# A hybrid encoder trunk: the input projection moved ahead and done in Strassen blocks

## Chip, cores and metric

The kernel runs on one core of a Trainium2 chip. The metric is device time in microseconds, as the median of three runs.

## What is computed

Two layers over 1024 tokens of 1024 features, float32. In each layer `h = RMSNorm(x)`, and one matrix product `proj = h @ w_in` (1024 x 6912) gives ten parts:

```
qA 512, kA 128, vA 128, zA 512, uB 512, vB 512, zB 512, qM 512, zM 512, gate logits 3 x 1024
yA = attention(rope(norm(qA)), rope(norm(kA)), vA) * silu(zA)      8 query heads of 64, 2 key heads, all 1024 keys
yB = uB * (W_s LayerNorm(vB) + b) * silu(zB)                       mixing within chunks of 128 tokens, 4 groups
yM = attention(qM, 256 memory keys and values) * silu(zM)          4 heads of 128
x  = x + (sum over n of sigmoid(gate_n) * (y_n @ w_br[n])) @ w_out  y_n 512 wide, w_br[n] 512 x 1024
```

After the last layer comes one more RMSNorm. The memory's keys and values are `RMSNorm(mem) @ w_mem_kv` in each layer.

## The kernel before

Every float32 operand is split into a high part (rounded to float32r) and a low part (the rest), and each product is three passes on TensorE, high x high, high x low, low x high (`mm3`, L107 to L110). The split takes a ScalarE copy and a VectorE subtraction (`split`, L112); for weights a ScalarE copy and, as a rule, GpSimd subtractions (`split_w`, L129). All DMAs go out on SyncE's queue.

The normed tokens stand transposed in SBUF as `hT`, 1024 features by 1024 tokens, high and low, in two token halves. A feature block of 128 columns is 8 K tiles x 3 passes of 512 tokens per half (`feat`, `feat_steps`); Q, K and V are made with rows as tokens and 256 weight columns moving (`token_proj`, `query`).

A layer runs in this order:

1. Branch A (`gqa`, L375): keys and values for the eight token tiles, then a loop over 32 units (key head, query tile, head pair) of four chunks each. A chunk `G` weighs values (`weigh`), turns the probabilities of chunk G+2 (`turn`), and in its second half computes scores and softmax of the unit after next (`scores`: product, maximum on VectorE, exponent on ScalarE, reciprocal on VectorE, scaling on GpSimd). Between them `fill` runs products that wait for nothing of the attention: the gate paths of branches A and B, kept in DRAM (`fillers`, L229). `owed` sets how many: 1.5 per chunk. The queries of the next tile are made in the same loop.
2. `merge` (L289): for each of 8 feature blocks the branch's output times `w_br`, into a two-bank tile `up = psS()`, of which there are two, and with it the tanh of the gate logits of a later block (`logits`, L275).
3. Branch M (`cross`, L622): memory keys and values, queries in the single bank `psM`, eight units of scores, turning, values; then its merge.
4. Branch B (`spatial`, L761), then its merge.
5. `out_proj` (L851), which for layer 0 also norms and turns the next layer's tokens.

The order on TensorE within an attention is that of the program (`in_order`); elsewhere a planner sets it by priorities. PSUM has two two-bank tiles `psS`, two banks `psT` for transposes, and one bank each `psM` and `psA`.

## Time and profile before

| What | Value |
|---|---|
| three runs, median (lowest to highest) | 2226.77 us (2225.23 to 2227.15) |
| profiled execution: span from first to last instruction | 2222.3 us (the page gives no other time for it) |
| TensorE busy | 2160.5 us, 97%, 11528 products |
| VectorE, ScalarE, GpSimd busy | 993.9, 865.3, 792.9 us |
| mean granted clock of TensorE | 0.998 |
| DMA | 133.61 MB, mean 60 GB/s |

A busy time is the union of an engine's instructions. TensorE's are pipelined: one lasts longer than the step to the next, so a busy TensorE isn't one at its peak, and the step has to be read from the starts. "Idle before" is the time that an engine stood still just before a group, with what ended it.

### The profile page before, as it was taken

To read this page: it belongs to the slowest core of one execution; us is meant where nothing else is said; L and a number is where in the kernel's file an instruction comes from. 1 tells how busy PE (TensorE), PEld (TensorE's weight loads), DVE (VectorE), ACT (ScalarE), POOL (GpSimd) and SP (SyncE) were. 2 spreads that over 40 slices of the span, in tenths; PEclk is the share of its full clock that TensorE was granted. 3 is DMA by queue.
4 is the path that set the end of the run, shared out by engine and by line. 5 is a ranking of instruction groups with operands and counts; after the bars stand their busy time and mean duration, and the time that the engine had idled before them with its cause. 6 is when DMAs were issued, how large, how long until landed. Compare 5 with 4: busy or idle time off the path is not lost.

```text
span 2222.3 us, 29304 instructions
## 1 busy us (share of the span) xinstructions
PE 2160.5 (97%) x11528; PEld 1844.7 (83%) x11528; DVE 993.9 (45%) x1670; ACT 865.3 (39%) x1679; POOL 792.9 (36%) x876
## 2 busy tenths in 40 slices
PE   8999999999999999999999999999999999999998
PEld 7889888788888888788788888888888888887887
DVE  6566676501334126414345676764013332264232
ACT  5566666511334111212245666664123341112132
POOL 6445454422133222422254454453221332223133
PEclk9999999999999999999999999999999999999999
DMA  4101010211211111312221110112123111212122
GB/s 167 53 29 40 28 39 20 95 48 57 77 47 58 48 54 34 122 47 97 94 87 39 38 39 25 39 34 77 47 66 90 31 55 46 58 67 95 41 100 78
DMA packets 111929, 133.61 MB, mean 60 GB/s; under 512 B 5168, under 2 KB 90160, under 8 KB 111792
## 3 DMA queue, kind: packets, MB, share of 16 engines
q1 hardware_dynamic: 111792, 131.75, 18.8%
q8 instruction: 90, 1.47, 0.3%
q14 instruction: 47, 0.39, 0.1%
HBM read 114.95 MB, written 16.78 MB: 59 GB/s over the span
## 4 chain that ended last, share of the span: by engine, by line
PE 84%; DVE 6%; ACT 4%; DMA 2%; POOL 2%; issue 2%; SPq 0%; POOLq 0%; ACTq 0%; DVEq 0%
PE psS L108 18%; PE psS L109 18%; PE psS L110 17%; PE psM L108 5%; PE psA L512 4%; PE psM L110 4%; PE psM L109 4%; PE psT L498 4%; PE psS L478 2%; PE psS L479 2%; DMA raw<-in_w_in_dram 1%; POOL wt L135 1%; ACT b L484 1%; DVE pT L115 1%; PE psA L108 1%
## 5 line engine op out<-in xcount | busy, mean ns | idle before, releaser
L135 POOL TENSOR_TENSOR wt<-raw,wt 128x512 fp32r<-128x512 f32 x286 | 385.0, 1370 | 704.8 <-ACT wt L132 703.1
L108 PE MATMUL psS<-hh,wt 128*128 128x512 f32 x896 | 354.4, 395 | 3.9 <-ACT th L286 3.9
L110 PE MATMUL psS<-hh,wt 128*128 128x512 f32 x896 | 350.3, 391 | 0.0
L109 PE MATMUL psS<-hl,wt 128*128 128x512 f32 x896 | 349.4, 390 | 0.0
L132 ACT CAST wt<-raw 128x1024 fp32r<-128x1024 f32 x164 | 172.3, 1053 | 323.2 <-PE psS L109 276.2
L108 PE MATMUL psS<-wt,hh 128*128 128x256 f32 (+1 forms) x736 | 253.7, 345 | 0.9 <-DVE th L318 0.6
L109 PE MATMUL psS<-wt,hh 128*128 128x256 f32 (+1 forms) x736 | 247.5, 336 | 0.5 <-POOL wt L135 0.5
L115 DVE TENSOR_TENSOR pT<-psT,pT 128x512 fp32r<-128x512 f32 x288 | 197.1, 687 | 112.1 <-ACT pT L114 111.2
L110 PE MATMUL psS<-wt,hl 128*128 128x256 f32 (+1 forms) x736 | 246.7, 335 | 0.0
L114 ACT CAST pT<-psT 128x512 fp32r<-128x512 f32 x288 | 167.9, 588 | 134.8 <-PE psT L498 96.3
L108 PEld LDWEIGHTS psS<-hh,wt 128*128 128x128 f32 x896 | 168.6, 188 | 44.9 <-ACT th L286 12.4
L286 ACT ACTIVATE th<-psS 128x512 f32<-128x512 f32 x96 | 57.2, 596 | 379.7 <-PE psS L110 379.7
L108 PE MATMUL psM<-hh,wt 128*128 128x512 f32 x480 | 195.8, 408 | 8.1 <-ACT th L263 6.7
L110 PEld LDWEIGHTS psS<-hh,wt 128*128 128x128 f32 x896 | 168.5, 188 | 36.2
L109 PEld LDWEIGHTS psS<-hl,wt 128*128 128x128 f32 x896 | 168.9, 188 | 33.1
L110 PE MATMUL psM<-hh,wt 128*128 128x512 f32 x480 | 188.2, 392 | 0.4 <-POOL wt L135 0.4
L109 PE MATMUL psM<-hl,wt 128*128 128x512 f32 x480 | 188.4, 392 | 0.0
L318 DVE SCALAR_TENSOR_TENSOR th<-th,psS 128x512 f32<-128x512 f32 x64 | 41.1, 684 | 312.7 <-PE psS L110 312.7
L486 POOL TENSOR_SCALAR b<-b,sums 128x1024 f32<-128x1024 f32 x128 | 144.3, 1128 | 98.8 <-DVE sums L485 83.8
L512 PEld LDWEIGHTS psA<-pT,b 128*128 128x128 f32 x1024 | 155.1, 190 | 26.1 <-DVE pT L115 4.4
L481 DVE TENSOR_REDUCE nm<-psS 128x1 f32<-128x1024 f32 x128 | 155.5, 1218 | 35.1 <-PE psS L479 34.9
L512 PE MATMUL psA<-pT,b 128*128 128x256 f32 x1024 | 165.7, 283 | 5.7 <-DVE pT L115 3.1
(191 smaller groups left out, 4009.2 us busy)
## 6 DMA issues: line engine op xcount, KB each, us to landing
raw<-in_w_in_dram SPq DMA_DIRECT2D x108, 512.0 KB, 3.8
raw<-in_w_br_dram SPq DMA_DIRECT2D x24, 512.0 KB, 3.4
raw<-in_w_mem_kv_dram SPq DMA_DIRECT2D x16, 512.0 KB, 3.5
raw<-in_w_out_dram SPq DMA_DIRECT2D x16, 512.0 KB, 3.7
b<-in_x_dram SPq DMA_DIRECT2D x12, 512.0 KB, 6.6
sz_a<-th SPq DMA_DIRECT2D x16, 256.0 KB, 2.7
uz_b<-th SPq DMA_DIRECT2D x16, 256.0 KB, 2.2
b<-sz_a SPq DMA_DIRECT2D x16, 256.0 KB, 3.7
```

Source lines behind the costliest of these rows:

```text
L108: in_order(nc.tensor.matmul(ps, sh, mh, start=start, stop=False))
L109: in_order(nc.tensor.matmul(ps, sh, ml, start=False, stop=False))
L110: in_order(nc.tensor.matmul(ps, sl, mh, start=False, stop=stop))
L114: nc.scalar.copy(h, src)
L115: nc.vector.tensor_tensor(out=l, in0=src, in1=f32(h), op=ALU.subtract)
L132: nc.scalar.copy(h, raw)
L135: op = lo_eng[0].tensor_tensor(out=l[:, k], in0=raw[:, k], in1=f32(h[:, k]), op=ALU.subtract)
L286: nc.scalar.activation(ts[th], gp[:, s], AF.Tanh, scale=0.5)
L481: nc.vector.tensor_reduce(out=nm, in_=S, axis=AX.X, op=ALU.max, negate=True)
L486: nc.gpsimd.tensor_scalar(out=p, in0=p, scalar1=sums, scalar2=1.0, op0=ALU.mult, op1=ALU.mult)
L498: in_order(nc.tensor.transpose(pt[:, (2 * j + h) * P:(2 * j + h + 1) * P], pp[k, h][:, kt * P:(kt + 1) * P], ident))
L512: in_order(nc.tensor.matmul(acc[:, :256], V[g][:, 2 * c + j], pv[:, j * 256:(j + 1) * 256], start=c + i + j == 0, stop=c == 3 and i + j == 2))
```

## The change

The whole input projection of a layer comes first. It takes two feature blocks (256 columns), both halves of K (b11, b21 hold the first token half, b12 and b22 the second) and both token halves as a 2 x 2 block matrix and makes seven products in place of eight. Differences of the tokens (t1 to t4) are made and split once per layer in `Tokens.put`, sums of weight quarters per pair in `combos`. A pair uses banks X, Y (one `psS`) and Z (`psM` or `psA`); two results are summed within a bank, others by VectorE from PSUM. The results go to DRAM. While the products run, `qkv` reads Q, K and V back for each token tile, turns, norms, rotates and stores them, and `spatial` does branch B; each `yield n` waits n products. Memory keys and values of both layers are made at the start. Then come the cross attention with branch B's projection as filler, the attention with branch M's, branch A's projection by itself, and the output projection. TensorE keeps the order of the program throughout (`pe`).

```diff
-FINISH = {70: (0, 0), 74: (1, 0), 78: (0, 1), 82: (1, 1), 116: (2, 0), 120: (3, 0)}
+FINISH = {110: (0, 0), 112: (1, 0), 115: (0, 1), 118: (1, 1), 121: (2, 0), 124: (3, 0)}
+ORDER = (1, 6, 2, 7, 5, 4, 3)
+EARLY = (1, 2, 6, 7, 5, 4, 3)
+MOVING = {1: "b11", 2: "b21", 3: "b22", 4: "t4", 5: "t1", 6: "t2", 7: "t3"}
+AHEAD = 7
+    slp = ctx.enter_context(tc.tile_pool(name="slp", bufs=16))
     wp = ctx.enter_context(tc.tile_pool(name="wp", bufs=8))
     rawp = ctx.enter_context(tc.tile_pool(name="rawp", bufs=2))
+    b2p = ctx.enter_context(tc.tile_pool(name="b2p", bufs=14))
+    def split_w(raw, lo=None):
+        w = wt([P, 2] + [int(n) for n in raw.shape[1:]])
+        tc.stamp_issue_order_token(nc.scalar.copy(w[:, 0], raw).ins, "cast")
+        (lo or nc.gpsimd).tensor_tensor(out=w[:, 1], in0=raw, in1=f32(w[:, 0]), op=ALU.subtract)
+        return w[:, 0], w[:, 1]
...
+    class Tokens:
...
+        def put(self, y, tt):
...
+            tensor(out=t3, in0=pts[1], in1=b12, op=ALU.subtract)
+            tensor(out=t1, in0=b12, in1=b11[0], op=ALU.subtract)
+            tensor(out=t1, in0=t1, in1=b11[1], op=ALU.subtract)
+            tensor(out=t2, in0=pts[1], in1=t1, op=ALU.subtract)
+            tensor(out=t4, in0=b21[0], in1=t2, op=ALU.subtract)
+            tensor(out=t4, in0=t4, in1=b21[1], op=ALU.add)
+            for name, t in (("t2", t2), ("t3", t3), ("t1", t1), ("t4", t4)):
+                h, l = self.get(name)
+                split(h[:, :, c], l[:, :, c], t, lo=nc.gpsimd)
+    def combos(raw, order):
...
+        a11, a12, a21, a22 = quad(0, 0), quad(0, 1), quad(1, 0), quad(1, 1)
...
+            elif p == 6:
+                s = slab((P, 4, 4, P), F32)
+                tensor(out=s[:, 0], in0=a21, in1=a22, op=ALU.add)
+                tensor(out=s[:, 1], in0=s[:, 0], in1=a11, op=ALU.subtract)
+                yield op(s[:, 1])
+            elif p == 7:
+                tensor(out=s[:, 2], in0=a11, in1=a21, op=ALU.subtract)
+                yield op(s[:, 2])
+            elif p == 5:
+                yield op(s[:, 0])
+            else:
+                tensor(out=s[:, 3], in0=a12, in1=s[:, 1], op=ALU.subtract)
+                yield op(s[:, 3])
+    class Block:
...
+        def product(self, p, w, h):
+            def mm(ps, start):
+                for k in range(4):
+                    mm3(ps, w[0][:, k], w[1][:, k], h[0][:, k], h[1][:, k], start and k == 0, k == 3, skip=True)
+            def add(ps, t, o):
+                with tc.high_priority(offset=400):
+                    nc.vector.tensor_tensor(out=o, in0=ps, in1=t, op=ALU.add)
+            if p == 1:
+                t = psS()
+                self.X, self.Y = t[:, :512], t[:, 512:]
+                mm(self.X, True)
+                self.c1 = b2()
+                with tc.high_priority(offset=400):
+                    nc.scalar.copy(self.c1, self.X)
+            elif p == 6:
+                mm(self.Y, True)
+                self.u2 = b2()
+                add(self.Y, self.c1, self.u2)
+            elif p == 2:
+                mm(self.X, False)
+                self.use(0, 0, self.X, True)
+            elif p == 7:
+                mm(self.Y, False)
+                self.u3 = b2()
+                add(self.Y, self.c1, self.u3)
+            elif p == 5:
+                zbank[0] = 1 - zbank[0]
+                self.Z = psM() if zbank[0] else psA()
+                mm(self.Z, True)
+                add(self.Z, self.u3, self.u3)
+                self.use(1, 1, self.u3, False)
+            elif p == 4:
+                mm(self.Y, False)
+                add(self.Y, self.c1, self.c1)
+                self.use(1, 0, self.c1, False)
+            else:
+                mm(self.Z, False)
+                add(self.Z, self.u2, self.u2)
+                self.use(0, 1, self.u2, False)
+    def in_proj(L, H, between, side):
+        seq = [(0, 1), (1, 1), (0, 2), (1, 2)]
+        seq += [(b, p) for b in (0, 1) for p in EARLY[2:]]
+        seq += [(b, p) for b in range(2, len(todo)) for p in ORDER]
...
+        for i, (b, p) in enumerate(seq):
+            prepare(i + 1 + AHEAD)
+            state[b].product(p, ops.pop((b, p)), H.get(MOVING[p]))
...
+    def branch(L, n, y, merged, first):
+        raws = [fetch(w_br[L.l, n], 0, 512, 4)]
+        for d0 in range(0, KT, 2):
+            W = [split_w(raws[-1][:, :, j * P:(j + 1) * P]) for j in (d0 % 4, d0 % 4 + 1)]
...
+            for th in range(2):
+                for j in range(2):
...
+                    dma(t, L.g[n * KT + d][:, half(th)])
+                    up = psM()
+                    for kt in range(4):
+                        mm3(up, wh[:, kt], wl[:, kt], y[th][0][:, kt], y[th][1][:, kt], kt == 0, kt == 3)
+                        if kt < 3:
+                            yield
...
+                    nc.vector.scalar_tensor_tensor(out=o, in0=t, scalar=1.0, in1=up, op0=ALU.add, op1=ALU.mult)
+                    if not first:
+                        nc.gpsimd.tensor_tensor(out=m, in0=m, in1=t, op=ALU.add)
+                    yield
+    def cross(L, fill):
...
+        for i in range(len(units) + 1):
+            if i < len(units):
+                scores(i, *q)
...
+            more(3)
+            if i:
+                parts = turned(i - 1)
+                more(3)
+                values(i - 1, parts)
+                more(2)
+    def attention(L, fill):
...
+        for G in range(4 * n):
+            k, c = divmod(G, 4)
+            weigh(G)
+            if G + 2 < 4 * n:
+                turned(G + 2)
+            if k + 2 < n and c >= 2:
+                scores(k + 2, c - 2)
...
+            if G % 8 in (0, 1, 3, 4, 6) or k + 2 >= n:
+                next(fill, None)
+    def out_proj(L, merged, x_src, half_done, done, after, resident):
...
+        def pair(i, cs=slice(0, D)):
+            xt[i] = slab((P, 2, D), F32) if resident else rawp.tile([P, 2, D], F32, name="raw", tag="raw")
+        side = [(4, tables(l))]
+        side += [(22 + 5 * tt, qkv(L, tt)) for tt in range(NT)]
+        side += [(64, spatial_consts(l))]
+        side += [(68 + 5 * tt, spatial(L, tt)) for tt in range(NT)]
+        in_proj(L, H, between, side)
...
+        ym = cross(L, branch(L, 1, yb, merged, True))
+        ya = attention(L, branch(L, 2, ym, merged, False))
+        for _ in branch(L, 0, ya, merged, False):
+            pass
```

## Rows read from the trace of the kernel before

**Rows 1.** The page: busy time of each engine, and the chain that ended last.

```profile
PE 2160.5 (97%) x11528; PEld 1844.7 (83%) x11528; DVE 993.9 (45%) x1670; ACT 865.3 (39%) x1679; POOL 792.9 (36%) x876
...
PE 84%; DVE 6%; ACT 4%; DMA 2%; POOL 2%; issue 2%; SPq 0%; POOLq 0%; ACTq 0%; DVEq 0%
```

**Rows 2.** Stages: window, its length, busy time by engine, clock, DMA share, GB/s.

```profile
0.00:20.00 20.00, 8.96 (x45) 8.00 (x46) 9.15 (x12) 11.18 (x19) 8.54 (x17) 1.00 0.83 302
...
84.00:430.00 346.00, 334.85 (x2131) 299.33 (x2132) 235.11 (x390) 220.15 (x440) 167.90 (x189) 1.00 0.12 36
430.00:560.00 130.00, 129.75 (x581) 106.50 (x580) 15.93 (x25) 25.52 (x37) 26.78 (x24) 1.00 0.20 61
560.00:880.00 320.00, 317.40 (x1580) 266.65 (x1579) 112.86 (x183) 89.09 (x176) 83.33 (x94) 1.00 0.17 52
880.00:1015.00 135.00, 132.75 (x591) 109.13 (x590) 52.15 (x78) 31.69 (x46) 43.47 (x34) 0.99 0.25 82
```

**Rows 3.** Groups of matrix products: busy us, mean ns | idle before.

```profile
L108 PE MATMUL psS<-hh,wt 128*128 128x512 f32 x896 | 354.4, 395 | 3.9 <-ACT th L286 3.9
...
L108 PE MATMUL psS<-wt,hh 128*128 128x256 f32 x384 | 115.4, 300 | 0.2 <-ACT hh L114 0.2
```

**Rows 4.** Timeline of PE: start us, length us, what; two places of layer 0.

```profile
480.26 0.39 PE L110 MATMUL psS<-hh,wt 128*128 128x512 f32 x1
...
486.83 0.39 PE L110 MATMUL psS<-b,wt 128*128 128x512 f32 x1
...
302.56 0.36 PE L108 MATMUL psS<-wt,hh 128*128 128x256 f32 x1
...
304.08 0.64 PE L512 MATMUL psA<-pT,b 128*128 128x256 f32 x4
304.56 0.60 PE L498 MATMUL psT<-identr,b 128*128 128x128 f32 x4
304.91 0.48 PE L478 MATMUL psS<-b,qS 128*128 128x512 f32 x1
...
305.92 0.40 PE L108 MATMUL psM<-hh,wt 128*128 128x512 f32 x1
```

**Rows 5.** Timeline about a single PSUM bank, the queries of the cross attention.

```profile
614.34 0.39 PE L110 MATMUL psM<-hh,wt 128*128 128x512 f32 x1
...
614.81 0.59 ACT L114 CAST qM<-psM 128x512 fp32r<-128x512 f32 x1
...
615.45 0.39 PE L694 MATMUL psS<-b,qM 128*128 128x256 f32 x1 [0.72 <-ACT qM L114]
```

**Rows 6.** Groups on DVE, ACT and POOL: busy us, mean ns | idle before.

```profile
L115 DVE TENSOR_TENSOR pT<-psT,pT 128x512 fp32r<-128x512 f32 x288 | 197.1, 687 | 112.1 <-ACT pT L114 111.2
L481 DVE TENSOR_REDUCE nm<-psS 128x1 f32<-128x1024 f32 x128 | 155.5, 1218 | 35.1 <-PE psS L479 34.9
...
L318 DVE SCALAR_TENSOR_TENSOR th<-th,psS 128x512 f32<-128x512 f32 x64 | 41.1, 684 | 312.7 <-PE psS L110 312.7
...
L485 DVE RECIPROCAL sums<-sums 128x1 f32<-128x1 f32 x128 | 20.3, 159 | 41.1 <-ACT b L484 39.9 <-POOL b L486 1.0
...
L484 ACT ACTIVATE b<-psS,nm 128x1024 f32<-128x1024 f32 x128 | 143.5, 1121 | 23.6 <-DVE nm L481 22.4
...
L484 ACT ACTIVATION_READ_ACCUMULATOR b<-psS,nm 128x1 f32 x128 | 25.2, 197 | 0.0
...
L135 POOL TENSOR_TENSOR wt<-raw,wt 128x512 fp32r<-128x512 f32 x286 | 385.0, 1370 | 704.8 <-ACT wt L132 703.1 <-PE psM L110 0.8
L486 POOL TENSOR_SCALAR b<-b,sums 128x1024 f32<-128x1024 f32 x128 | 144.3, 1128 | 98.8 <-DVE sums L485 83.8 <-issue 6.6 <-PE psM L110 4.5
```

**Rows 7.** Timeline of DVE, then of POOL, in layer 0's merge of branch B.

```profile
954.24 1.29 DVE L319 TENSOR_TENSOR b<-b,th 128x512 f32<-128x512 f32 x2
...
970.65 3.29 DVE L319 TENSOR_TENSOR b<-b,th 128x512 f32<-128x512 f32 x2
...
970.41 2.98 POOL L135 TENSOR_TENSOR wt<-raw,wt 128x512 fp32r<-128x512 f32 x2 [18.42 <-ACT wt L132]
```

More of the change, by code (lines that the diff above doesn't have):

```diff
@@ L566, in gqa @@
                 scores(k, hh)
-                for _ in range(2):
-                    next(fill)
-        turn(0)
-        turn(1)
-        ask = None
-        owed = 0.0
-        more = ahead(fine=True)
+                if k + hh < 2:
+                    next(fill, None)
+        turned(0)
+        turned(1)
         for G in range(4 * n):
@@ new lines, in out_proj, with load, rows @@
+                split(h[:, kt % 4], l[:, kt % 4], merged[kt // 2][:, kt % 2, half(th)], 0.5)
+        xt = {}
+        def load(c):
+            W = []
+            for k0 in (0, 4):
+                raw = fetch(w_out[L.l], c * 512, 512, 4, k0)
+                W += [split_w(raw[:, i]) for i in range(4)]
+            return W
+        def rows(i):
+            return slice(2 * i * P, (2 * i + 2) * P)
+        def pair(i, cs=slice(0, D)):
+            xt[i] = slab((P, 2, D), F32) if resident else rawp.tile([P, 2, D], F32, name="raw", tag="raw")
+            dma(xt[i][:, :, cs], x_src[rows(i), cs].rearrange("(i p) d -> p i d", p=P))
@@ new lines, in products, with add @@
+        def products(op, tt, W, kts):
+            t = slice((tt % 4) * P, (tt % 4 + 1) * P)
+            for kt in kts:
+                h, l = mT[tt // 4][kt // 4]
+                wh, wl = W[kt]
+                mm3(op, h[:, kt % 4, t], l[:, kt % 4, t], wh, wl, kt == 0, kt == KT - 1)
+        def add(op, x):
+            nc.vector.tensor_tensor(out=x, in0=op, in1=x, op=ALU.add)
+        W = load(0)
+        for th in range(2):
+            if resident:
+                pair(2 * th)
+                pair(2 * th + 1)
+            banks = [b for _ in range(2) for b in (lambda q: (q[:, :512], q[:, 512:]))(psS())]
+            for kt in range(KT):
+                for i in range(4):
+                    products(banks[i], 4 * th + i, W, [kt])
+            for i in range(4):
+                tt = 4 * th + i
+                if resident:
+                    x = xt[tt // 2][:, tt % 2, :512]
+                else:
+                    x = b2()
+                    dma(x, x_src[tt * P:(tt + 1) * P, :512])
+                add(banks[i], x)
+                half_done(tt, x)
+                if not resident:
+                    dma(x_mid[tt * P:(tt + 1) * P, :512], x)
@@ new lines, in out_proj @@
+        W = load(1)
+        bank = []
+        for tt in range(NT):
+            if not bank:
+                q = psS()
+                bank = [q[:, :512], q[:, 512:]]
+            if not resident and tt % 2 == 0:
+                pair(tt // 2, slice(512, D))
+                dma(xt[tt // 2][:, :, :512], x_mid[rows(tt // 2), :512].rearrange("(i p) d -> p i d", p=P))
+            op = bank.pop(0)
+            products(op, tt, W, range(KT))
+            x = xt[tt // 2][:, tt % 2]
+            add(op, x[:, 512:])
+            done(tt, x)
+            after(tt)
@@ new lines, in trunk, with take_x, norm_x, put_x @@
+    H = Tokens()
+    gb = wt((P, D), F32)
+    x0 = {}
+    def take_x(i):
+        s = slab((P, 2, D), F32)
+        dma(s, x_in[0, 2 * i * P:(2 * i + 2) * P].rearrange("(i p) d -> p i d", p=P))
+        x0[2 * i], x0[2 * i + 1] = s[:, 0], s[:, 1]
+    def norm_x(tt):
+        rms_rows(x0[tt], gb)
+    def put_x(tt):
+        H.put(x0.pop(tt), tt)
+    mems = [memory(0), memory(1)]
+    next(mems[0])
+    get_kv()
+    dma(gb, norm_g[0].partition_broadcast(P))
+    take_x(0)
+    get_kv()
+    take_x(1)
```

1242 lines of the change are left out of this document (553 added, 689 removed).

## Prediction

> **What bounds the kernel now.** I read the page first. TensorE is busy 97% of the 2222.3 us span, the next engine 45%, and the chain that ended last lies on TensorE for 84% [rows 1]. Cut into stages, TensorE idles in two places only: about 11 us in the first 20 us, and 11.2 us of the 346 us in which layer 0 does its attention; the dense stretch behind it idles 0.25 us in 130 [rows 2]. So the time is a count of matrix products times the step from one to the next. The listed mean durations overlap and can't be added: a 512-column product lasts 395 ns [rows 3], but in the timeline 29 of them start within 486.83 - 480.26 = 6.57 us, a step of 0.2266 us [rows 4]. From the same group: twelve 256-column products take 304.08 - 302.56 = 1.52 us, four 256-column value products 0.48, four transposes 304.91 - 304.56 = 0.35, the four 512-column score products of one softmax tile 305.92 - 304.91 = 1.01.
>
> Three timed runs have a median of 2226.77 us. The page gives the profiled execution its span and no other time; the sum below is made on the span, and 4.5 us (median less span) are put on at the end.
>
> **What goes.** The input projection has 54 feature blocks of 128 columns. Of these 48 run as 512-column products: 48 blocks x 8 K tiles x 2 token halves = 768 triples per layer, 1536 in both, of which [rows 3] shows the largest group, 896. 1536 x 3 x 0.2266 = 1044.2 us. The other six blocks (Q, K, V) run with 256 moving columns, 384 triples [rows 3], which are 96 twelves: 96 x 1.52 = 145.9 us. Together 1190.1 us.
>
> **What comes in its place.** 27 pairs of blocks, 7 products of 4 K tiles x 3 passes: 84 products of 512 columns a pair, 4536 in both layers, 1027.9 us. The output is now features by tokens, so Q, K, V (six per token tile) and the spatial values (four) are turned: 160 transposes, 40 x 0.35 = 14.0 us. All other products keep count and shape. TensorE's work falls by 1190.1 - 1027.9 - 14.0 = **148.2 us**. Were nothing else late, the time would be about 2078 us. What follows is what I expect to be late.
>
> **One bank for the branch projections: +59 us.** Before, `merge` takes `psS`, two buffers, and the logits stand between two groups. After, `branch` takes `psM`, one buffer: the next group of 12 products can't start before VectorE has read the last. The nearest case is the single bank of the cross queries [rows 5]: last product starts 614.34, the reader starts 614.81 and takes 0.59, the next product starts 615.45. That is 1.11 us where the plain step is 0.23, so 0.88 us are lost; with the reader of this change (0.684, [rows 6]) 0.98. It counts wherever two groups follow each other with nothing between. For branch A, which runs after the attention with nothing beside it, that is 15 places per layer. In the cross attention the steps come in runs of 3, 3 and 2, and every border of four steps falls inside a run: 15 again. In the attention other work (0.8 us or more) lies between, which I count as cover. 60 x 0.98 = 58.8 us. Below: 45, if some of it falls where TensorE would wait anyway. Above: 95, if the reader often stands behind another VectorE instruction.
>
> **Attention without projections beside it: +38 us.** A unit of the attention loop is 4 x (0.48 + 0.35) + 2 x 1.01 = 5.3 us of TensorE. Before, about 6 us of gate products per unit stretch it to 10.8 us (346 / 32). After, the filler is only branch M, 64 steps of 0.68 us: 5 in 8 chunks, so 1.7 us per unit until chunk 98 of 128, then none. VectorE's work per unit is 4 x 0.687 + 2 x (1.218 + 0.159) = 5.5 us, ScalarE's 4 x 0.59 [rows 5] + 2 x (1.121 + 0.197) = 5.0 before the copies of the finished unit [rows 6]: three engines near 6 to 7 us. What is late next is the softmax. From the second tile's scores to its first transpose the order leaves 0.68 + 0.84 + 0.84 + 0.68 + 0.48 = 3.5 us of TensorE work with filler and 2.2 without. The chain in that time is 1.218 + 1.121 + 0.197 + 0.159 + 1.128 = 3.82 us [rows 6] and about 0.45 of hand-overs (0.47 less the step, and 0.05 each, from [rows 5]): 4.27. So 0.77 us wait per unit in the first 24.5 units and 2.07 in the next 5.5 (the last two have no scores): 18.9 + 11.4 = 30.3 us per layer, less the 11.2 that the stage idles now. Both layers: 38 us. Below: -22, if the waits vanish and the present idle too. Above: every chain stands 1.25 us in queues on top, 24.5 x 2.0 + 5.5 x 3.3 - 11.2 = 56 us per layer, 112 in both.
>
> **The projection itself: +24 us.** A pair takes 19.0 us of TensorE. GpSimd has seven splits of 1.37 us [rows 6] in it (9.6), VectorE four sums of weight quarters (0.645 each when nothing disturbs, [rows 7]) and five sums from PSUM (0.684): 6.0 us. That hides easily, and a bank is read one whole product (2.7 us) before it is needed again. In products 22 to 110 the normalising and turning of Q, K and V and the spatial branch run beside it: per token tile, in 13.6 us, some 7 us more of VectorE (eleven 512-column instructions at 0.645, the narrower K part) with 0.71 x 6.0 and the SiLU products (1.0 to 2): 13 of 13.6 us. TensorE waits in order for the turned q. No row shows this mix; between 0 (it fits) and 43 us per layer (rival C) I take 12 per layer, near the lower end, because weights are made seven products ahead.
>
> **Ends.** Start: TensorE now loses 11 us in 20 [rows 2]; after, it must wait for the memory rows and norm, then does both layers' memory keys and values while x is prepared: +10 (-5 to 30). Between the layers the raw weights share two buffers with x: the second block's weights can be fetched only when the last token tile has been turned, so a fetch, a cast and a split of 1.37 us [rows 6] are late with nothing beside them; of the fetch no row is shown here, and I take +8 in all (0 to 25). Idle of the old cross and spatial stages that goes: 2.60 and 2.25 us per layer [rows 2], -10 in both. Some 76 MB of stores to DRAM come in (38 MB per layer, counted from the shapes in the code) and are read back; the transfer engines are 12 to 25% busy behind the start [rows 2], and I count nothing for them. If the loads of the turned tiles come late, that is in the projection's upper bound.
>
> **Sum.** 2222.3 - 148.2 + 58.8 + 38 + 24 + 10 + 8 - 10 = 2202.9; with 4.5 around it **2207 us**, 0.9% below the median.
>
> **Rivals.**
> *A. It stays fed.* Softmax and projection cost nothing net: 2207 - 38 - 24 = 2145. For it: VectorE and ScalarE are at 68% and 64% in today's attention, and [rows 2] shows TensorE at 97% with them. Against: the lead of 3.5 us is shorter than the bare chain of 4.27.
> *B. The attention is set by the softmax chain (slower).* The place is the transpose that waits for GpSimd's scaling; the price is the upper bound above, 112 in place of 38: 2281. It decides from 10 us per layer beyond my sum, 0.33 us per unit, that is from a chain of about 4.6 us. For it: balanced engines queue. Against: whenever TensorE waits, the other engines catch up.
> *C. The projection is set by VectorE and GpSimd together (slower).* A VectorE instruction with two SBUF inputs takes 0.645 us alone, but two took 3.29 us while GpSimd worked, and GpSimd's own pair 2.98 where 2 x 1.37 is the mean [rows 6, 7]: they take turns, and a VectorE one that meets GpSimd loses 3.29 / 2 - 0.645 = 1.0 us. If six of the 16 such instructions per token tile do (GpSimd is busy half of the time), VectorE lacks 6.0 - 0.6 = 5.4 us in 13.6; eight tiles make 43 us per layer, 86 in place of 24: 2269. For it: those splits of 1.37 us never end. Against: a wait of TensorE lets weights run ahead and GpSimd fall idle. The Trainium skill, SBUF — State Buffer, section SBUF: two separate sides, states the rule behind that row: the port pair that the two share is "an exclusive lock, not a bandwidth split", and the loser waits for the whole instruction. The trace agrees (3.29 us for the pair).
>
> *D. The saving is not there.* If the sums between the seven products hold their banks, TensorE waits about 2 us a pair, 54 x 2 = 108 us, in place of 24: 2291. Against it: 2.7 us of other products stand between.
>
> **Chances.** Forecast 0.50 (own range 2165 to 2250), A 0.20, B 0.16, C 0.10, D 0.04. Within the forecast's range, about 0.36 lies faster by over 0.2% (which is about what can be told from no change), 0.05 within, 0.09 slower; A is faster; of B, C and D 0.05 faster, 0.02 the same, 0.23 slower. Faster 0.61, same 0.07, slower 0.32. The range reaches from somewhat below A to B: 2130 to 2285.
>
> **What would show it.** Right: the 512-column products fall by 4608 - 4536 = 72 and step by 0.227, the 256-column ones fall by 1152; in branch A a wait of about 1 us on VectorE's reading every 3.7 us; in the attention waits on GpSimd's scaling, and a stage of 235 to 250 us; the projection at 540 to 550 us per layer. Wrong: an attention stage of 265 us or more (B), TensorE waiting for transposed rows or weights in products 22 to 110 for over 30 us per layer (C), waits on the five sums (D), or none of it (A).

## The result and the profile after

The changed kernel takes 2748.27 us (median of 4 runs, 2741.89 to 2753.0) against 2226.17 us before: 1.234 times as long, 95% interval 1.2319 to 1.236. The forecast was 2207 us with a range to 2285, so it was wrong, and by far.

First the page, the lines that answer to [rows 1]: busy time of each engine, and the chain that ended last.

```profile
span 2751.2 us, 29839 instructions
PE 2238.9 (81%) x10464; PEld 1793.6 (65%) x10464; DVE 1326.5 (48%) x1990; ACT 1032.4 (38%) x2053; POOL 1127.2 (41%) x1092
...
PE 13%; ACT 3%; DVE 3%; POOL 2%; issue 1%; DMA 1%; POOLq 0%; SPq 0%; DVEq 0%; ACTq 0%
```

TensorE issues 11528 - 10464 = 1064 products fewer, which is what was forecast (1152 + 72 fewer, 160 transposes more), yet it stands still for 512 us. The chain line can't be set beside that of [rows 1]: there the shares add up to 100%, here to 23%, so the chain was followed back over the last 23% of the span only. Of those 23, TensorE has 13. No other engine is above half busy. So no engine has become the bound: TensorE waits, in small pieces, for engines that are idle most of the time.

The stages of layer 0, the same view as [rows 2] (window, length, busy time of PE, PE's weight loads, DVE, ACT, POOL, each with its instructions, granted clock, DMA share, GB/s): start, projection while queries, keys and the spatial branch are prepared beside it (the mixed stretch), projection of the gate logits with no preparation beside it (the quiet stretch), cross attention, attention, last branch.

```profile
0.00:136.00 136.00, 78.41 (x477) 73.97 (x478) 76.34 (x89) 61.93 (x116) 67.58 (x66) 0.80 0.48 164
...
252.00:600.00 348.00, 259.67 (x1070) 204.89 (x1071) 197.35 (x320) 102.58 (x206) 132.82 (x121) 0.86 0.37 115
600.00:860.00 260.00, 231.95 (x977) 180.99 (x976) 75.60 (x100) 84.35 (x141) 106.81 (x82) 0.99 0.36 118
860.00:959.00 99.00, 80.97 (x408) 64.36 (x407) 43.76 (x71) 34.79 (x98) 26.23 (x42) 0.98 0.55 186
959.00:1256.00 297.00, 251.43 (x1475) 209.75 (x1474) 185.72 (x285) 182.19 (x364) 132.15 (x151) 0.97 0.15 47
1256.00:1320.00 64.00, 49.52 (x192) 35.73 (x191) 23.55 (x34) 15.69 (x28) 29.62 (x24) 0.97 0.23 75
```

The granted clock is to be seen too: 0.86 in the mixed stretch, 0.80 at the start, where before no stage of [rows 2] was under 0.99. A mean of 0.931 over the span means that 2 x 0.069 x 2751 = 380 us ran at the lower level, 1.2 GHz; before it was 0.998. Of the stages shown it is lowest in the two in which TensorE stands idle most (42% and 25%, in pieces of up to 10.2 us); the last branch, idle for 23% in waits of about 1 us, had 0.97.

Counting each stage's products at their step (0.2266 us for 512 columns, [rows 4]; 0.12 and 0.09 for the small ones) and taking that from its length gives what is lost, to waits and to the lower clock together. Stages are cut at the starts of products in the trace.

| Stage | length, us | lost, us | lost by the forecast |
|---|---|---|---|
| start | 136.4 | 82 | 21 |
| projections, both layers, with the layer change in the second | 726.0 + 748.9 | 400 | 32 |
| attentions | 296.5 + 298.0 | 177 | 61 |

Those three rows are 545 us over the forecast, and the span is 2751.2 - 2202.9 = 548 over it, so what the other stages are off by nearly cancels. Next, who ended TensorE's waits: the list of waits of the changed kernel (total us, times, longest).

```profile
PE psS L107 <- DVE b L298: 89.2, 54, 7.3
PE psS L107 <- ACT b L306: 84.9, 42, 10.2
PE psT L112 <- POOL s L783: 59.4, 55, 2.6
PE psS L107 <- DVE b L118: 39.9, 12, 7.6
PE psM L107 <- DVE b L650: 38.3, 42, 1.9
PE psM L107 <- DVE s L650: 35.6, 30, 3.2
```

The groups view has the same on the products themselves, as [rows 3] has it of before (busy us, mean ns | idle before, by whom):

```profile
L107 PE MATMUL psS<-s,wt 128*128 128x512 f32 x1080 | 470.9, 436 | 229.8 <-DVE b L298 89.2 <-ACT b L306 84.9 <-ACT b L398 17.6
L108 PE MATMUL psS<-s,wt 128*128 128x512 f32 x1080 | 450.9, 417 | 0.0
```

The idle time stands before L107, the first of each three passes, where [rows 3] had 3.9 us on its largest group. The first two waits are the projection's: L298 is `add`, the sum of two products, L306 the copy of the first product. L783 is the scaling of the softmax, L118 the low half of a split (at the start, memory keys and values), L650 the single branch bank.

The timeline of the quiet stretch (start, length, engine, line) shows how the first two come about. A product is 12 instructions; only the last and first of each are shown.

```profile
708.84 0.39 PE L109 MATMUL psS<-s,wt 128*128 128x512 f32 x1
...
709.26 0.58 ACT L306 COPY b<-psS 128x512 f32<-128x512 f32 x1 [1.36 <-PE psS L109]
...
709.90 0.50 PE L107 MATMUL psS<-s,wt 128*128 128x512 f32 x1 [0.68 <-ACT b L306]
...
712.53 0.39 PE L109 MATMUL psS<-s,wt 128*128 128x512 f32 x1
...
713.01 0.69 DVE L298 TENSOR_TENSOR b<-psS,b 128x512 f32<-128x512 f32 x1 [0.35 <-PE psS L109]
...
713.75 0.50 PE L107 MATMUL psS<-s,wt 128*128 128x512 f32 x1 [0.84 <-DVE b L298]
...
716.81 0.60 ACT L398 ACTIVATE b<-psS 128x512 f32<-128x512 f32 x1 [3.19 <-PE psS L109]
...
717.46 0.50 PE L107 MATMUL psS<-s,wt 128*128 128x512 f32 x1 [0.69 <-ACT b L398]
```

At 708.84 the last instruction of product 1 starts, into X. The next, product 6, writes Y, the other bank, and yet starts only when the copy of X has ended. At 713.75 product 2 goes to X and waits for the sum that reads Y. At 717.46 product 7 goes to Y and waits for the tanh that reads X. Each time the reader and the writer use different banks, but the banks are halves of one tile (`t = psS(); self.X, self.Y = ...`), so the wait goes by the tile (the first experiment tests it). About 1 us, three times in the 84 products of a pair of blocks.

In the mixed stretch the copy itself is late:

```profile
289.89 0.69 DVE L481 TENSOR_TENSOR b<-b,b 128x512 f32<-128x512 f32 x1
291.38 0.69 DVE L482 TENSOR_TENSOR b<-b,rstd 128x512 f32<-128x512 f32 x1 [0.80 <-POOL rstd L127]
292.11 0.71 ACT L117 CAST b<-b 128x256 fp32r<-128x256 f32 x2 [4.04 <-DVE b L482]
...
292.73 0.58 ACT L306 COPY b<-psS 128x512 f32<-128x512 f32 x1
293.36 0.79 PE L107 MATMUL psS<-s,wt 128*128 128x512 f32 x1 [10.19 <-ACT b L306]
```

ScalarE idles 4.04 us in front of a cast of the rotated query, whose VectorE chain is not done; the copy stands behind that cast in ScalarE's queue though its product ended long before; TensorE idles 10.19 us.

### The profile page after: what moved, and what is told of

It is laid out like the page before. It is cut to its first block, busy times and chain, and to the rows that moved or that the text cites. A ratio compares the mean times of both kernels' runs of the same rounds, so it can differ in the third digit from the quotient of the medians.

```text
span 2751.2 us, 29839 instructions
## 1 busy us (share of the span) xinstructions
PE 2238.9 (81%) x10464; PEld 1793.6 (65%) x10464; DVE 1326.5 (48%) x1990; ACT 1032.4 (38%) x2053; POOL 1127.2 (41%) x1092
## 5 line engine op out<-in xcount | busy, mean ns | idle before, releaser
L107 PE MATMUL psS<-s,wt 128*128 128x512 f32 (+1 forms) x1144 | 493.7, 432 | 244.7 <-DVE b L298 89.2
L149 POOL TENSOR_TENSOR wt<-s,wt 128x512 fp32r<-128x512 f32 x216 | 288.6, 1338 | 463.0 <-ACT wt L148 462.2
L109 PE MATMUL psS<-s,wt 128*128 128x512 f32 (+1 forms) x1144 | 469.7, 411 | 3.8 <-POOL wt L149 3.8
L108 PE MATMUL psS<-s,wt 128*128 128x512 f32 (+1 forms) x1144 | 472.5, 413 | 0.0
L107 PEld LDWEIGHTS psS<-s,wt 128*128 128x128 f32 x1144 | 235.8, 206 | 345.2 <-DVE b L298 110.5
L298 DVE TENSOR_TENSOR b<-psS,b 128x512 f32<-128x512 f32 x162 | 111.6, 689 | 457.9 <-PE psS L109 355.5
L148 ACT CAST wt<-raw 128x512 fp32r<-128x512 f32 x274 | 168.6, 619 | 420.1 <-PE psS L109 229.9
L107 PE MATMUL psM<-s,wt 128*128 128x512 f32 x600 | 253.3, 422 | 74.5 <-DVE b L650 38.3
L118 DVE TENSOR_TENSOR b<-psT,b 128x512 fp32r<-128x512 f32 x288 | 194.8, 689 | 185.8 <-ACT b L117 174.5
L112 PE MATMUL psT<-identr,s 128*128 128x128 f32 x1248 | 209.4, 289 | 86.9 <-POOL s L783 59.4
L109 PEld LDWEIGHTS psS<-s,wt 128*128 128x128 f32 x1144 | 236.1, 206 | 56.4 <-POOL wt L149 5.5
L108 PEld LDWEIGHTS psS<-s,wt 128*128 128x128 f32 x1144 | 237.0, 207 | 42.0 <-POOL s L118 0.2
L108 PE MATMUL psM<-s,wt 128*128 128x512 f32 x600 | 238.1, 397 | 0.4 <-DVE s L121 0.4
L109 PE MATMUL psM<-s,wt 128*128 128x512 f32 x600 | 237.8, 396 | 0.0
L117 ACT CAST b<-psT 128x512 fp32r<-128x512 f32 x288 | 165.1, 587 | 142.6 <-PE psT L112 140.4
L803 PE MATMUL psA<-b,s 128*128 128x256 f32 x1024 | 188.1, 299 | 17.0 <-DVE b L118 15.3
L803 PEld LDWEIGHTS psA<-b,s 128*128 128x128 f32 x1024 | 158.3, 194 | 56.1 <-DVE b L118 25.6
L107 PEld LDWEIGHTS psM<-s,wt 128*128 128x128 f32 x600 | 114.7, 191 | 121.4 <-DVE b L650 53.9
L783 POOL TENSOR_SCALAR s<-s,sums 128x1024 f32<-128x1024 f32 x128 | 144.5, 1130 | 105.5 <-DVE sums L782 93.8
```

The lines of the kernel that those rows point to most:

```text
L107: pe(nc.tensor.matmul(ps, sh, mh, start=start, stop=False, skip_group_check=skip))
L108: pe(nc.tensor.matmul(ps, sh, ml, start=False, stop=False, skip_group_check=skip))
L109: pe(nc.tensor.matmul(ps, sl, mh, start=False, stop=stop, skip_group_check=skip))
L112: pe(nc.tensor.transpose(out, in_, ident if idn is None else idn))
L117: nc.scalar.copy(h, src)
L118: lo.tensor_tensor(out=l, in0=src, in1=f32(h), op=ALU.subtract)
```

## The experiments

The kernel before took 2226 to 2228 us in every group of runs, so the runs can be set beside each other; each is the median of 2 to 11 executions that lie within 0.6% of each other. "The changed kernel" is the one above, 2748 us.

### X and Y in tiles of their own

```diff
-                t = psS()
-                self.X, self.Y = t[:, :512], t[:, 512:]
+                self.X = psS()[:, :512]
...
             elif p == 6:
+                self.Y = psS()[:, :512]
                 mm(self.Y, True)
```

> The quadrant sums X and Y, halves of one two-bank tile in the changed kernel, get a tile each; nothing else changes. Theory 1 (TensorE stands because a product that writes one half waits for the reader of the other half, about 1.0 us three times a pair of blocks): the pair in the logits stretch falls from 22.1 to 19.1-19.4 us, the projection stage from 724 to 600-660 us a layer, the time from 2748 to 2540-2620 us. Rival (the readers themselves are late, behind other work on ScalarE and VectorE, and the product that needs their result waits for them all the same): the quiet pair stays above 21.5 us and the time above 2720 us. In between, 2640-2700 us: the quiet stretch is mended and the one with the attention preparation beside it is not, so that has its own cause.

Measured 2580.23 us, 168 less. The projections fell to 644.6 and 667.6 us. The last ten pairs (840 products) of layer 0's projection, first in the changed kernel, then here, in the windows view:

```profile
638.72:862.35 223.63, 199.50 (x842) 155.20 (x840) 63.73 (x83) 72.75 (x121) 92.03 (x70) 1.00 0.37 125
```

```profile
584.84:778.76 193.92, 190.86 (x841) 157.42 (x840) 64.63 (x83) 73.35 (x122) 95.45 (x71) 1.00 0.42 144
```

22.4 us a pair become 19.4; the products alone need 84 x 0.2266 = 19.0. So the shared tile accounts for all but 0.4 us of what a quiet pair lost, and the rival is out there. The stretch with the preparation beside it kept some 66 us of waits a layer, a cause of its own.

### Casts queued later

```diff
+        yield 1
         tabk, tabq = tabs[0]
...
         k = rope(kr[:, :P], tabk, 2, tt, ...)
+        q = rope(qr, tabq, 8, tt, (b2(), b2()))
+        yield 2
         ks = b2(F32R, (P, 2, 2, 2, 64))
```

> The preparation of queries and keys issues its two rope chains first and the ScalarE casts that read their results two products later, so that the casts are queued behind the copy of the first product and not ahead of it. X and Y stay halves of one tile. Theory 2 (in-order queues: the copy of the first product stands behind casts that wait for VectorE): the waits on that copy in the stretch from 252 to 600 us fall from 35 us a layer to under 10, the time by 40-70 us to 2680-2710 us. Rival (VectorE and GpSimd are slowed by each other, so the work is late wherever it is queued): the stretch keeps its length within 10 us and the time stays at 2735-2760 us.

Measured 2660.67 us, 87.6 less, somewhat more than expected. The work that took the 348 us of the mixed stretch takes some 42 us less a layer (projections 683.6 and 706.2 us), the quiet stretch is unchanged (222.9 us for ten pairs). The waits on the copy fell from 84.9 us to 49.8 in all, in the mixed stretch from 33 to 15 or 16 us a layer, not to under 10:

```profile
PE psS L107 <- ACT b L306: 49.8, 44, 6.3
```

### Eight plain products in place of seven

```diff
-ORDER = (1, 6, 2, 7, 5, 4, 3)
+ORDER = ((0, 0, 0), (0, 0, 1), (0, 1, 0), (0, 1, 1), (1, 0, 0), (1, 0, 1), (1, 1, 0), (1, 1, 1))
...
+            if k == 0:
+                self.bank[j, th] = psS()[:, :512] if j == 0 else (psA() if th else psM())
```

> The seven products with their sums are replaced by the plain eight products of the quadrants; stages, DRAM buffers, side work and the strict order on TensorE stay, each quadrant sum has a bank of its own. TensorE gets 54 x 12 matmuls more, 147 us at 0.2266 us each. If the sums of the seven products cause the long projection (theory 1 and what hangs on it): the quiet pair is 21.8-22.2 us, the projection stage 600-640 us a layer instead of 724, and the time 2500-2580 us, faster than with seven products. Rival (the side work beside a strictly ordered projection is what costs, with seven or with eight): the stage is 724 us or longer, the time 2740-2900 us.

Measured 2515.58 us: 233 less than seven products, with 147 us more work on TensorE. Projections 629.2 and 633.3 us for 27 x 96 x 0.2266 = 587 us of products. The windows rows of layer 0's projection and of its last ten pairs:

```profile
108.58:737.82 629.24, 617.54 (x2839) 510.77 (x2837) 149.08 (x280) 175.13 (x340) 189.65 (x172) 1.00 0.41 135
518.69:737.82 219.13, 217.76 (x962) 180.03 (x960) 0.00 (x0) 47.62 (x82) 51.69 (x41) 1.00 0.28 98
```

A quiet pair takes 21.9 us, as expected, and VectorE has nothing at all to do in it. The same preparation lies beside both, started every 6 products instead of every 5, so the staging as such costs at most 42 us a layer here. The rest goes with what only the seven products need. That is more than their sums and the tile that they share: GpSimd splits four weights a pair instead of seven (189.65 us of work in the projection against 301), and the differences of the tokens go, with which the start falls from 136.4 us to 108.6. This run doesn't part them.

### Attention, last branch and start, one edit each

```diff
-            if k + 2 < n and c >= 2:
-                scores(k + 2, c - 2)
+            if k + 2 < n and 1 <= c <= 2:
+                scores(k + 2, c - 1)
...
-                    up = psM()
+                    up = psA() if alone and (th + j) % 2 else psM()
...
-            pair = psS()
...
-                ps = pair[:, j * 512:j * 512 + 256]
+                ps = psS()[:, :256]
```

> Three edits in three stages, projection untouched: scores of the unit after next are issued one step earlier in the attention; the last branch uses two banks in turn; the two halves of a memory key or value product at the start get a tile each. If the attention is set by the latency of the softmax chain against its lead (rival B of the prediction): 297 us falls to 255-270 us a layer. If a rate of ScalarE, VectorE or GpSimd sets it: it stays within 8 us. Last branch: 64 us falls to 48-52 us a layer if its waits are the single bank's. Start: 136 us falls to 100-115 us if it waits for the halves; it stays if it waits for casts queued behind the norm chain. All three: 2590-2650 us.

Measured 2638.07 us, 110 less. Start, attention, last branch of layer 0:

```profile
0.00:119.40 119.40, 73.56 (x480) 69.74 (x481) 80.20 (x89) 60.77 (x116) 68.81 (x66) 0.83 0.55 187
933.40:1193.90 260.50, 237.58 (x1472) 201.54 (x1471) 184.13 (x285) 182.41 (x363) 131.65 (x151) 1.00 0.16 54
1193.90:1253.00 59.10, 49.19 (x194) 37.75 (x195) 24.22 (x35) 15.47 (x27) 28.66 (x24) 0.94 0.24 83
```

The attention fell by 36 us a layer with the same work on every engine, so what went was the lead of the scores over the softmax chain being too short, and no rate. The start gave 17 us. The last branch gave only 5 to 8: by `(th + j) % 2` the groups take the banks in the order M, A, A, M, and at a repeat the wait is still there (0.78 and 1.42 us at two that follow each other). With the column half alone (`j`, next runs) it is 48.0 us.

### Apart and later; apart and spread

> X and Y in tiles of their own and the casts of queries and keys two products later, both. The first run with X and Y apart took 2580 us, with 66 us of waits and 22 us of half clock a layer left where the attention preparation runs beside the products. If these are the copy queued behind casts that wait (theory 2), the waits there fall to 25-40 us and the time to 2490-2540 us. If the delay of the copy is already covered by the product that now lies between it and its user, and the sums on VectorE are late by themselves: 2560-2585 us.

Measured 2484.04 us, 96 less than apart alone: as much as the later casts gave by themselves, so the two causes add. A copy that comes late still holds its user, one product between or not.

```diff
-        side += [(22 + 5 * tt, qkv(L, tt)) for tt in range(NT)]
+        side += [(22 + 9 * tt, qkv(L, tt)) for tt in range(NT)]
...
-        side += [(68 + 5 * tt, spatial(L, tt)) for tt in range(NT)]
+        side += [(102 + 9 * tt, spatial(L, tt)) for tt in range(NT)]
```

> X and Y apart, and the same preparation of queries, keys and the spatial gate started every 9 products instead of every 5, so that it lies beside the whole projection; its instructions and their order inside a unit are unchanged. If each unit of it costs TensorE a fixed wait (a queue that stands behind a chain): the waits only move, 2560-2590 us. If the wait comes from how dense the work of VectorE, GpSimd and ScalarE is beside the products: the 66 us a layer fall to 20-40 us, with the lost clock 2470-2520 us.

Measured 2555.83 us, 24 less than apart alone. That lies between the two expectations, 4 us under the first: here most of the loss goes with each unit of preparation and not with how dense the units lie.

### All mends, on seven and on eight products

> All the mends together on seven products: X and Y apart, casts later, preparation spread, scores one step earlier, two banks in turn (now really in turn, by the column half alone) in the first and the last branch with the cross sums in a transposes' bank, memory halves apart, eight banks in turn in the output projection. From 2580 us of X and Y apart: attention -73, last branch -26, first branch -16, start -16, output projection -25 give 2424 us, less 40-90 us for the projection's preparation: 2335-2385 us if the causes add up. If they stand in for each other, above 2424 us. Faster than before (2227 us) only if more than 200 us of waits go that no run has shown yet.

Measured 2327.95 us, a little under the expected range: the causes add up.

> The same mends outside the projection on the plain eight products (2516 us): attention -73, last branch -26, first branch -16, start -16, output projection -25: 2360 us, 2340-2385 us. Beside the seven products with all mends this tells what the seventh saves once its waits are mended: TensorE's work says 147 us, so if the seven are clean they win by 100 us or more; if the two come out within 40 us, the sums of the seven still cost what they save.

Measured 2363.34 us, as expected. The seven win by 35 us of the 147 that they save, within the 40 that were to mean that their sums still cost what they save. The comparison isn't even: the casts queued later and the spread preparation are in the seven alone.

### Even dealing in the attention, shorter chains

```diff
         k = rope(kr[:, :P], tabk, 2, tt, ...)
+        yield 1
...
+        yield 1
         vh, vl = b2(F32R), b2(F32R)
...
-            if G % 8 in (0, 1, 3, 4, 6) or k + 2 >= n:
+            if G % 4 in (0, 3) or G % 12 == 5 or k + 2 >= n:
```

> All mends on seven products (2328 us) with two more. The branch's products beside the attention are dealt out where no scores are issued, two steps in four and one more in twelve, until they last to the attention's end, instead of five steps in eight in a pattern that takes no account of the scores. The chains of keys, queries and the gate's norm are cut by one product more each, so that sums need not stand behind a whole chain. If the attention's last 52 us of waits a layer are steps in which too little work covers the turning of a chunk: 261 us falls to 235-245 us a layer, and the projection's waits from 43 to 30 us: 2255-2300 us. If the chunk's chain sets the step in any case: 258-262 us stay, 2310-2330 us. Before stands at 2228 us; under that only if nearly all waits go.

Measured 2272.04 us. The attention takes 239.8 and 241.8 us, so most of its last waits were steps with too little work beside them. That is the stage I had forecast (235 to 250), reached with two edits that the change doesn't have. The projections fell by 6 and 9 us a layer, less than the 13 expected of the cut chains.

> The same without spreading: the preparation starts every 5 products again. If, with the casts queued later, density is what is left (VectorE operations of 0.68 us run up to 1.8 us beside GpSimd), this is 30-70 us longer than the spread one. If spreading only moves fixed waits, the two agree within 10 us.

Measured 2272.38 us, the same as spread: once the casts are late enough, spreading moves waits.

> As the spread one, but the copy of the first product goes to VectorE, where the sums that use it stand, and so leaves ScalarE's queue with its casts. The waits named after that copy were 22 us in all. If the queue is the cause they go and 10-25 us with them; if VectorE is the bound beside the projection, its sums come later by the copy's 0.6 us each and the time is the same or longer by up to 20 us.

Measured 2288.67 us, 17 more. The 22 us of waits on the copy were those of the kernel of 2328 us; in the one of 2272 us 3.0 us were left, so there was little to gain. On VectorE the copy is waited for 23.0 us and the sums 27.7 instead of 43.3, so VectorE's queue had become the tighter one.

> The plain eight products with all mends and the even dealing in the attention: 2363 us less 30-50 us as the attention gains, 2313-2335 us. Against the seven products with the same mends this prices the seventh product in a mended schedule: 147 us of TensorE work less what the sums still make it wait; about 35-60 us expected.

Measured 2327.26 us; seven products win by 55. By stages, their projections are 72 us shorter in both layers together (1188 against 1260 us), and their start is 25 us longer (121.4 against 96.6), as it makes the differences of the tokens.

### Start and layer change

```diff
-                ps = psS()[:, :256]
+                ps = (psS, psM, psS, psA)[(2 * n + j) % 4]()[:, :256]
...
-                if tt:
-                    H.put(rows.pop(tt - 1), tt - 1)
+                if tt in (2, 4):
+                    get_raw(tt // 2 - 1, l + 1, *layers[l + 1][1:])
+                if tt > 1:
+                    H.put(rows.pop(tt - 2), tt - 2)
...
+                x = b2(), b2()
```

> The spread kernel with all mends (2272 us) and the two seams mended: the memory products at the start take their banks in turn from all four that are idle there; at the layer change the residual rows are held in the small buffers instead of the two weight buffers, the next layer's first weights are fetched during the output projection, and the turning of normed rows goes one row further behind. If start and layer change are latencies and buffers held too long: start -8 to -14 us, layer change -15 to -22 us, 2238-2250 us. If the rate of ScalarE, VectorE and GpSimd sets them: within 6 us of 2272 us.

Measured 2288.96 us, 17 more instead of 23 to 36 less. The start did what was expected (121.4 to 109.9 us). The layer change did not: at 1141 us TensorE waits 12.5 us for an addition in the output projection, which itself waits for its residual row ("<-DMA b<-in_x_dram" on four additions in a row, 3 to 6 us each): the rows now share the small buffers, and in SyncE's queue each load stands behind the store before it. The next projection begins 4.6 us later after the attention and lasts 14.5 us longer, as two rows are turned inside it.

> The same seams on the dense preparation (every 5 products, 2272 us): the same -23 to -36 us, 2236-2250 us, as the seams lie outside the preparation.

Measured 2283.47 us, 11 more: the same.

### The weights' low parts on VectorE

```diff
-        op = split_w
+        op = lambda r: split_w(r, nc.vector)
```

> As e13, but the low parts of the weights in the projection (378 subtractions, 1.3 us each on GpSimd) are made on VectorE at 0.68 us, some 130 us of VectorE a layer more in 500. If the two engines slowing each other is what makes the sums late: VectorE's operations return to 0.68 us, the projection's waits fall from 30 to under 20 us a layer, and the time is 10-30 us below e13. If VectorE's queue as such is the bound: the waits grow, 20-80 us above e13.

Measured 2218.65 us, 70 less than the same kernel with GpSimd making them, more than twice what was expected, and for the first time less than before (ratio 0.996, 0.9944 to 0.9976). VectorE's groups (mean ns), first with GpSimd:

```profile
L297 DVE TENSOR_TENSOR b<-psS,b 128x512 f32<-128x512 f32 x162 | 111.1, 686 | 239.3 <-PE psS L109 231.4 <-issue 7.7
L281 DVE TENSOR_TENSOR s<-raw,s 128x512 f32<-128x512 f32 x54 | 66.9, 1239 | 0.7
...
L480 DVE TENSOR_TENSOR b<-b,rstd 128x512 f32<-128x512 f32 x16 | 23.5, 1471 | 3.4 <-POOL rstd L127 3.2
```

then without it:

```profile
L149 DVE TENSOR_TENSOR wt<-s,wt 128x512 fp32r<-128x512 f32 x216 | 150.8, 699 | 46.4 <-ACT wt L148 45.6
...
L297 DVE TENSOR_TENSOR b<-psS,b 128x512 f32<-128x512 f32 x162 | 111.4, 688 | 126.6 <-PE psS L109 126.2
...
L281 DVE TENSOR_TENSOR s<-raw,s 128x512 f32<-128x512 f32 x54 | 38.6, 715 | 0.4
...
L480 DVE TENSOR_TENSOR b<-b,rstd 128x512 f32<-128x512 f32 x16 | 10.9, 681 | 1.2 <-POOL rstd L127 1.2
```

Instructions with two SBUF inputs go from 1239 and 1471 ns to 715 and 681 (the groups of that kind that changed most; some were not slowed at all); the sums, with one input from PSUM, took 686 before and 688 after. The sums were not slow. They stood behind slow ones: TensorE's waits on those in psS, first with GpSimd, then without, are

```profile
PE psS L107 <- DVE b L297: 43.4, 26, 6.1
PE psS L107 <- DVE b L297: 11.8, 12, 1.6
```

The edit also takes the subtractions out of GpSimd's queue, in front of its other work. The durations show that VectorE was slowed; what the shorter queue gave by itself no run shows.

> The changed kernel with one edit: the low parts of the projection's weights are made on VectorE instead of GpSimd. X and Y stay halves of one tile, the casts stay where they were. If the two engines slowing each other is a cause of its own size, the stretch with the preparation beside it shortens from 348 us by 30-60 us a layer and the time from 2748 to 2630-2690 us. If it mattered only once the other waits were gone: 2720-2760 us. If VectorE is too full for it beside the sums: over 2760 us.

Measured 2693.81 us, 54.5 less, and so just outside the expected 2630 to 2690: the projections became 26 and 29 us shorter, not 30 to 60. The cause is there in the changed kernel too, a little smaller than expected.

### The best of it

> The spread seven products with all mends, the weights' low parts on VectorE, the banks at the start in turn, and the layer change as the changed kernel has it. 2219 us less the 18 us by which the edited layer change was longer: 2195-2208 us, against 2228 us before: faster, ratio 0.985-0.992.

Measured 2208.39 us, at the upper end of what was expected, ratio 0.9924 (0.9911 to 0.9938): 0.8% less than before. Start, projection, attention and last branch of layer 0:

```profile
0.00:108.90 108.90, 71.42 (x481) 67.66 (x481) 79.74 (x89) 58.28 (x112) 64.15 (x61) 0.87 0.58 198
108.90:664.60 555.70, 544.82 (x2512) 449.64 (x2513) 401.41 (x707) 226.72 (x424) 68.25 (x68) 1.00 0.48 153
754.70:994.50 239.80, 229.11 (x1473) 200.40 (x1472) 184.46 (x285) 180.46 (x363) 131.78 (x151) 1.00 0.18 59
994.50:1042.50 48.00, 45.19 (x194) 35.76 (x194) 24.00 (x35) 15.15 (x27) 27.77 (x23) 1.00 0.30 102
```

Its TensorE issues the same 10464 instructions as the changed kernel's; 2748 and 2208 us are two orders and placements of the same products. That 2208 is next to the forecast of 2207 is chance: this kernel has a second branch bank and an earlier softmax, which the forecast had not, and it loses time at the start and to the clock, which the forecast had not counted.

> The same with the preparation every 5 products. Spread and dense agreed within 6 us where GpSimd had the weights; with VectorE holding 0.7 us more a weight, the dense stretch has less room on it: equal to the spread one or up to 30 us longer, 2195-2235 us.

Measured 2231.26 us, 23 more than spread, within the range but not equal. With VectorE holding the weights' parts, density does matter.

## Why the prediction was wrong

**TensorE's work, -148 us: right.** The counts fell as forecast, the step stayed at 0.227 us at full clock.

**One branch bank, +59 us: right.** The two lines on L650 are 72 waits of 1.03 us, 73.9 us, where 60 of 0.98 us (58.8) were forecast, and under the upper bound of 95. Two banks in turn took the last branch from 64.4 us to 48.0.

**The projection, +24 us: the step that failed.** "A bank is read one whole product (2.7 us) before it is needed again" is true of each bank and false of the tile that two of them share. Rival D asked whether a sum holds its own bank; what held was the neighbour's reader, in a kernel whose order on TensorE is fixed, so nothing else could run meanwhile. The first experiment prices it at 168 us; the stages took 726 and 749 us where 540 to 550 were the mark. The code that showed it, `self.X, self.Y = t[:, :512], t[:, 512:]`, was before me.

The second part that failed: VectorE's and GpSimd's work was summed against the time ("13 of 13.6 us"), with no account of order. The timeline at 290 us shows ScalarE's queue served in order: a copy that TensorE needs waits for a cast that waits for a chain. Queuing the casts later gave 88 us alone and 96 behind the first mend. Rival C's mechanism, 86 us by the forecast, measured 54.5 alone and 70 at the end; its mark did not come, as TensorE waited some 12 us for transposed rows in layer 0's mixed stretch and for weights not at all, but 62 us for the copies and the sums. The Trainium skill (SBUF — State Buffer, section SBUF: two separate sides) says that a VectorE instruction with two SBUF inputs is shut out while a GpSimd instruction that reads SBUF holds the ports that they share. The runs agree: 1239 ns beside GpSimd's subtractions and 715 without, and the sums from PSUM at 686 and 688.

**Attention, +38 us: rival B came.** The mark was 265 us, the stage took 296.5 and 298.0. The lead of 3.5 us against a chain of 4.27 was the right comparison, and the chain was the term sized too small: it was the sum of bare durations and hand-overs. One unit's second tile, from the start of its last score product to the end of its scaling (1060.49 + 2.22):

```profile
1057.63 0.39 PE L774 MATMUL psS<-s,b 128*128 128x512 f32 x1
...
1058.05 1.22 DVE L776 TENSOR_REDUCE nm<-psS 128x1 f32<-128x1024 f32 x1 [0.34 <-PE psS L774]
...
1059.02 1.07 ACT L117 CAST b<-psT 128x512 fp32r<-128x512 f32 x2
...
1059.97 1.13 ACT L781 ACTIVATE s<-psS,nm 128x1024 f32<-128x1024 f32 x1
...
1060.49 2.22 POOL L783 TENSOR_SCALAR s<-s,sums 128x1024 f32<-128x1024 f32 x2
```

That is 5.1 us, and the exponent stands behind two casts of turned probabilities. Over all 64 units the mean is 5.6 us; counted as in the forecast, from one step later and with the last hand-over, some 5.5 instead of 4.27. In the kernel before the same stretch has a mean of 5.3 us, so it could have been read there. Besides, the filler was not where the waits are. Issuing the scores one step earlier gave 73 us in both layers, dealing the filler evenly brought the stage to 240.

**Ends.** The start loses 82 us where 21 were counted. The shared tile of the memory products is 17 us of it, and a further 11.5 came from more banks. Some 25 us are the differences of the tokens, a term that the forecast put at nothing: with eight products, which need none, the start is 108.6 us instead of 136.4 and, in the mended kernels, 96.6 instead of 121.4 (those runs also order their first products otherwise). At the layer change the first casts of weights and the turned rows cost TensorE 19 us of waits in 1436 to 1470 us; my attempt to mend it failed, so its cause is open.

**The clock was not priced.** Frequent short waits went with 380 us at 1.2 GHz. By the steps inside those stretches some 116 us were lost to it, an estimate that is part of the losses above; no run tries the clock by itself, but it came back as the waits went (mean 0.941 apart, 0.957 apart and later, 0.981 at the end).

**The rivals were put as alternatives and came together.** B, C and D had chances of 0.16, 0.10 and 0.04, each with the rest of the sum kept. B came, C's mechanism came, and D's mark, waits on the sums, came by another mechanism. Added, their prices give 2207 + 74 + 62 + 84 = 2427. The range ended at B's 2281, below D's own 2291. Even the sum is 321 us short of what was measured: the prices were too small as well, and the start and the clock were in none of them.

Not settled: how much of the seven products' saving their sums still eat. Seven were ahead of eight by 35 and 55 us of 147 in mended kernels with GpSimd on the weights, and there the eight lacked the mends of the preparation; eight products with these, or with the weights on VectorE, were not tried.

## What to carry to other kernels

When the order on an engine is written out by hand, look at every tile that two of its neighbours share and at every instruction queued ahead of a reader it waits for; a sum of busy times that fits shows neither. Rivals that sit in different stages are not alternatives: add their prices for the slow end of the range. If products are saved by making more sums, price the engine that makes the sums by its queue and by what shares its ports, not by its busy share.

## What was not expected of the hardware

Beside GpSimd's subtraction of weights (1338 to 1374 ns) groups of VectorE instructions with two SBUF inputs had means up to 2.2 times as long (1471 against 681 ns), while every group that reads PSUM kept its mean within 11 ns. Giving GpSimd's work to the busiest engine behind TensorE (VectorE, from 335 to 402 us in the projection of layer 0) made the changed kernel faster by 54.5 us, and the mended one by 70. And TensorE had a mean granted clock of 0.931 with no idle piece longer than 10.2 us on the list of its waits.
